# The last quarter of a merged product turned by token tile, and the loads around it: a hybrid encoder block on one core

## The chip, the cores and the metric

The kernel runs on one core of one Trainium2 chip, for a batch of 1, 256 tokens and a width of 2048, all in float32. The metric is the device time of one execution in microseconds (us), lower is better. The engines are PE (matrix multiply, with PEld for its weight loads), DVE (VectorE), ACT (ScalarE), POOL (GpSimd, which here only issues DMAs) and SP (SyncE, which issues the loads of the weights). DMAs that ACT issues have a queue of their own too.

## The reference

One encoder block: two branches work side by side on the projected input (a gated linear attention, GLA, and a Hyena long convolution), sigmoid gates merge them, one product and a LayerNorm follow, then a squared-ReLU MLP and a second LayerNorm. The change lies between the merge and the first LayerNorm.

```python
proj = h @ w_in[l]
q, k, v, r, af, ab, hy_u, gate_logits = jnp.split(proj, split_idx, axis=-1)
y_gla = _gla_branch(q, k, v, r, af, ab, ...)
y_hy = _hyena_branch(hy_u, ...)
g = jax.nn.sigmoid(gate_logits).reshape(B, L, N_BRANCH, D)
merged = g[:, :, 0, :] * (y_gla @ w_gla_o[l]) + g[:, :, 1, :] * (y_hy @ w_hy_o[l])
mix = merged @ w_out[l]
h = _layernorm(DEEPNORM_ALPHA * h + mix, ln1_g[l], ln1_b[l])
ff = jnp.square(jax.nn.relu(h @ w_ff1[l])) @ w_ff2[l]
h = _layernorm(DEEPNORM_ALPHA * h + ff, ln2_g[l], ln2_b[l])
```

## The kernel before

Every large product is made of weight blocks of 128 x 2048 numbers (1 MB). `fetch` (line 115) loads a block on SP's queue into one of three `raw` tiles and splits it in two halves into a high and a low part: the high part `whi` is a cast on ACT (line 108), the low part `wlo` a subtraction on DVE (line 109). There are three slots each for halves of `whi` and `wlo`. Activations are kept as high and low parts as well, and three matmuls (high by high, high by low, low by high) make one exact product. `next_block` fetches one block and hands out an earlier one, so that two blocks are on their way.

`token_group` (line 215) makes one group of 512 output columns for both token tiles (tb = 0 and 1, of 128 tokens each): four blocks, each with four slices of the contraction, and for each slice three matmuls for tb = 0 and three for tb = 1, which is 96 matmuls in a group. After each block it calls `pump`. `later(d, fn)` (line 135) puts work aside until d more blocks have gone by; `pump` then runs it, and `drain` runs all that is left.

The place of the change is the product with `w_hy_o`, the groups ho0 to ho3 of lines 822 to 833. Each group is merged with the gates: a multiplication (line 828) and an addition (line 829) for each token tile on DVE. The result has tokens on the partitions, and the next product, with `w_out` (groups wo0 to wo3, lines 904 to 910), needs channels there, so it is turned: DVE transposes blocks of 32 x 32 (line 203), one DMA from POOL's queue writes the 512 KB of the group to DRAM (`bounce_out`, line 207, tensor tr_m), and four DMAs from the same queue read it back in the turned order (`bounce_in`, line 213, tile mg, 128 KB each). `back_split` (line 817) splits the tile mg into the high and low parts of mT, on ACT and DVE. For ho0 to ho2 this split is put aside for two blocks; for ho3 it comes at once, by `drain` on line 834, and so stands in the program ahead of the first block of wo0. The fourth block of each wo group reads the quarter of mT that ho3 gives.

Behind it the program loads x into z1 (line 842, 2 MB in one DMA) and the two LayerNorm rows, broadcast to all partitions, into rows1 (`load_rows`, lines 844 to 848 and 893, two DMAs of 1 MB), all on ACT's queue. They lie in the place that yhT (the input of the ho groups) had, so they can't start before the last ho matmul is done. `add_mix` (line 895) reads z1 after each wo group, and rows1 is read from line 930 on. Lines 957 to 1006 are an order written out by hand for the LayerNorm. `load_rows(2)` on line 1062, behind `ff1(0)`, loads the rows of the second LayerNorm into the same tile.

The order of the instructions on each engine is not that of the program text: a planner goes through a simulated time, and gives an engine that is free the earliest instruction of the program whose inputs are ready by its estimates. What it has put in line stays in line on the chip. `tc.high_priority()` moves instructions ahead of others that are ready at the same time.

Of the kernel before, what the change touches and what calls it, by code (L numbers as in the profile page):

```python
# [10 lines left out]
F32 = mybir.dt.float32  # L11
# [3 lines left out]
ALU = mybir.AluOpType  # L15
DRAM = bass.MemoryType.DRAM

P = 128
D = 2048
L = 256  # L20
NT = L // P
# [38 lines left out]
def block_kernel(  # L60
# [23 lines left out]
    nc = tc.nc  # L84
# [10 lines left out]
    base = ctx.enter_context(tc.tile_pool(name="base", bufs=1))  # L95
# [39 lines left out]
    def later(d, fn):  # L135
        clock[1] += 1
        side.append((clock[0] + d, clock[1], fn))
# [9 lines left out]
    def drain():  # L147
        for e in sorted(side, key=lambda e: e[:2]):
            e[2]()
        side.clear()  # L150
# [51 lines left out]
    def turn_blocks(st, src):  # L202
        nc.vector.transpose(st, src.rearrange("p k (b i) -> p b k i", b=4))  # L203

    def bounce_out(name, st, n):
        td = drp.tile([n, P, 512], F32, tag=f"tr_{name}", name=f"tr_{name}")
        nc.gpsimd.dma_start(td.rearrange("t p x -> p t x"), st)  # L207
        return td

    def bounce_in(sg, td):  # L210
        src = td.rearrange("t (a i) (b x) -> b i (t a) x", a=4, b=4)
        for b in range(4):
            nc.gpsimd.dma_start(sg[32 * b:32 * b + 32], src[b])

    def token_group(act, name):
        pss = [psum_main(f"{name}_{tb}") for tb in range(NT)]
        for b in range(4):
            token_products(pss, act, [next_block()], range(NT), b)
            pump()
        return pss  # L220
# [28 lines left out]
    dfth = base.tile([P, 4, P], F32R, tag="dfth", name="dfth")  # L249
    dftl = base.tile([P, 4, P], F32R, tag="dftl", name="dftl")  # L250
# [11 lines left out]
    with tc.tile_pool(name="xp", bufs=1) as xp:  # L262
# [26 lines left out]
        for g in range(4):  # L289
            pieces = 2 if g == 0 else 1  # L290
            for b in range(OPENING):
                if g % 2 == 0:
                    halves_of[b] = weight_half(b, g // 2)
                hi, lo = halves_of[b]
                n = pieces if b == 0 else 1
                w, step = 512 // n, 4 // n
                for i in range(n):
                    at = 512 * (g % 2) + w * i
                    cs = slice(512 * g + w * i, 512 * g + w * (i + 1))
# [150 lines left out]
    pa = open_ps[0]  # L450
# [18 lines left out]
    for g in range(4):  # L469
        ng = fp.tile([P, 512], F32, tag="ng", name=f"ng{g}")  # L470
        nc.scalar.dma_start(ng, norm_g[0:1, g * 512:(g + 1) * 512].broadcast_to([P, 512]))
        pss = token_group(xT, f"r{g}")
# [181 lines left out]
    def m_part(g, tb):  # L654
        return m_sb[g // 2][:, tb, (g % 2) * 512:(g % 2 + 1) * 512]
# [160 lines left out]

    def back_split(dst, sg):
        src = sg.rearrange("p a (k j) -> p k a j", k=4)
        hi, lo = (dst[:, :, i].rearrange("p k (a j) -> p k a j", a=8) for i in range(2))
        split_hi_lo(hi, lo, src)  # L820

    for g in range(4):
        pss = token_group(yhT, f"ho{g}")
        st = hp.tile([P, NT, 512], F32, tag=("Z", "pa")[g % 2], name=f"mt{g}")
        for tb in range(NT):
            gp2 = g2_sb[:, tb, g * 512:(g + 1) * 512]
            mp = m_part(g, tb)
            nc.vector.tensor_tensor(gp2, gp2, pss[tb], op=ALU.mult)
            nc.vector.tensor_tensor(mp, mp, gp2, op=ALU.add)
            turn_blocks(st[:, tb].rearrange("p (b k j) -> p b k j", b=4, k=4), mp.rearrange("p (k x) -> p k x", k=4))  # L830
        sg = hp.tile([P, 8, P], F32, tag=("Tl", "pb")[g % 2], name=f"mg{g}")
        bounce_in(sg, bounce_out(f"m{g}", st, NT))
        later(2, lambda g=g, sg=sg: back_split(mT[:, 4 * g:4 * g + 4], sg))
    drain()
    hstk.close()
    qkg.close()

# [1 line left out]
    ep = ctx.enter_context(tc.tile_pool(name="ep", bufs=1))  # L839
    zr = base.tile([P, 4, D], F32, tag="yT", name="zr")  # L840
    z1 = zr[:, 0:2]
    nc.scalar.dma_start(z1, x.rearrange("(a p) d -> p a d", p=P))

    def load_rows(i0):
        rows = zr[:, 2:4]
        for i in range(2):
            nc.scalar.dma_start(rows[:, i, :], ln_rows[i0 + i:i0 + i + 1, :].broadcast_to([P, D]))
        return rows
# [41 lines left out]
                            MM(ps, sl, hi[:, cs], start=False, stop=(kt == KT - 1))  # L890

    st1 = ep.tile([P, NT, 8, 6], F32, tag="bst", bufs=2, name="bst1")
    rows1 = load_rows(0)

    def add_mix(ps, tb, at, n):
        zc = z1[:, tb, at:at + n]
# [338 lines left out]
```

## Time and profile before

| what | value |
|---|---|
| median of 3 runs | 1858.11 us (1857.54 to 1872.73) |
| profiled execution, its own time | 1857.15 us |
| its span in the trace | 1855.3 us |
| PE busy | 1834.9 us, 99% of the span |
| DVE busy | 1311.4 us, 71% |
| ACT busy | 913.8 us, 49% |
| POOL busy | 177.7 us, 10% |
| moved by DMA | 411.64 MB, 222 GB/s on average |

The profile is one execution. Busy times of the engines overlap, so they don't add up to the span. The chain of waits follows the work that ended last back from the end of the execution, and the windows give the busy time of each engine, the granted clock of PE (1.00 is full speed) and the load of the DMA engines in a stretch. Times within the execution are counted from the start of the span.

### The profile page before, as it was taken

Reading aid. Unit: us, or ns where it says so; the run is one execution under the profiler, and the core shown is the slowest. Engines: PE = TensorE matmul, PEld = TensorE weight load, DVE = VectorE, ACT = ScalarE, POOL = GpSimd, SP = SyncE. Lnnn points to the kernel's source line nnn. Section 1 sums busy time; section 2 is a strip of 40 time slices with the busy share of each in tenths; the row PEclk is TensorE's granted clock in tenths of the full one; section 3 lists DMA queues with packets and bytes.
Section 4 is the critical chain, followed back from the end, with each engine's and each line's share of the span. In section 5 each row is a group of like instructions: output and inputs, shape, how many; then the busy total and the mean of one; then the engine's idle time right before and its main releaser. Section 6 shows DMA issues by size and latency. Waiting matters only on the chain.

```text
span 1855.3 us, 22858 instructions
## 1 busy us (share of the span) xinstructions
PE 1834.9 (99%) x8732; PEld 1531.8 (83%) x8732; DVE 1311.4 (71%) x1660; ACT 913.8 (49%) x1152; POOL 177.7 (10%) x316
## 2 busy tenths in 40 slices
PE   8999999999999999999999899999999999999998
PEld 6888888888888888888888687888888888888887
DVE  6778878985798899898756566666655655565567
ACT  5555547665555555555544344444434443444332
POOL 1000000031111121121101100011100100010000
PEclk9999999999999999999999999999999999999999
DMA  8667665457666676676666863677755765676553
GB/s 283 217 231 283 241 241 184 176 182 238 220 222 232 221 258 228 228 243 239 231 215 227 309 214 116 243 234 245 235 196 197 248 226 191 221 233 222 187 197 120
DMA packets 73582, 411.64 MB, mean 222 GB/s; under 512 B 10912, under 2 KB 13632, under 8 KB 34048
## 3 DMA queue, kind: packets, MB, share of 16 engines
q1 hardware_dynamic: 47376, 324.03, 48.6%
q0 software_dynamic: 19328, 66.88, 11.8%
q10 hardware_dynamic: 6768, 19.27, 3.0%
q8 instruction: 68, 1.11, 0.2%
q14 instruction: 42, 0.34, 0.1%
HBM read 375.01 MB, written 35.13 MB: 221 GB/s over the span
## 4 chain that ended last, share of the span: by engine, by line
PE 59%; issue 4%; DMA 3%; DVE 2%; POOL 1%; ACT 0%; DVEq 0%; ACTq 0%; POOLq 0%
PE w L93 19%; PE f L93 18%; PE g L93 5%; PE go L93 4%; PE wo L93 3%; PE ux L93 2%; PE uz L93 2%; PE uv L93 2%; DMA tr_m<-mt 1%; PE ho L93 1%; PE Zp L93 1%; PE yp L93 1%; DMA mg<-tr_m 1%; PE wo L49 0%; PE f L49 0%
## 5 line engine op out<-in xcount | busy, mean ns | idle before, releaser
L109 DVE TENSOR_TENSOR wlo<-raw,whi 128x1024 fp32r<-128x1024 f32 (+2 forms) x603 | 726.2, 1208 | 408.6 <-ACT whi L108 398.2
L108 ACT CAST whi<-raw 128x1024 fp32r<-128x1024 f32 (+2 forms) x603 | 628.0, 1043 | 710.1 <-PE w L93 185.1
L93 PE MATMUL w<-whi,f 128*128 128x512 f32 x960 | 296.1, 389 | 0.0
L93 PE MATMUL f<-whi,hT 128*128 128x512 f32 x960 | 296.1, 389 | 0.0
L93 PEld LDWEIGHTS f<-whi,hT 128*128 128x128 f32 x960 | 180.2, 188 | 37.4
L93 PEld LDWEIGHTS w<-whi,f 128*128 128x128 f32 x960 | 180.2, 188 | 37.4
L93 PE MATMUL f<-wlo,hT 128*128 128x512 f32 x480 | 186.7, 389 | 0.0
L93 PE MATMUL w<-wlo,f 128*128 128x512 f32 x480 | 186.7, 389 | 0.0
L93 PE MATMUL g<-whi,xT 128*128 128x512 f32 x512 | 158.3, 389 | 0.0
L93 PEld LDWEIGHTS g<-whi,xT 128*128 128x128 f32 x512 | 96.1, 188 | 20.0
L93 PEld LDWEIGHTS w<-wlo,f 128*128 128x128 f32 x480 | 90.1, 188 | 18.7
L93 PEld LDWEIGHTS f<-wlo,hT 128*128 128x128 f32 x480 | 90.1, 188 | 18.6
L93 PE MATMUL g<-wlo,xT 128*128 128x512 f32 x256 | 99.9, 390 | 0.0
L93 PE MATMUL r<-whi,xT 128*128 128x512 f32 x256 | 82.3, 391 | 0.0
L93 PE MATMUL v<-whi,xT 128*128 128x512 f32 x256 | 80.1, 390 | 0.0
L93 PE MATMUL go<-whi,yg 128*128 128x512 f32 x256 | 79.8, 389 | 0.0
L93 PE MATMUL ho<-whi,yh 128*128 128x512 f32 x256 | 79.0, 389 | 0.0
L93 PE MATMUL wo<-whi,mT 128*128 128x512 f32 x208 | 67.0, 401 | 5.0 <-ACT whi L108 3.7
L93 PE MATMUL uz<-xT,whi 128*128 128x512 f32 x256 | 65.0, 392 | 0.0
L93 PE MATMUL uv<-xT,whi 128*128 128x512 f32 x256 | 64.8, 391 | 0.0
L93 PE MATMUL ux<-xT,whi 128*128 128x512 f32 x256 | 64.6, 392 | 0.0
L207 POOL DMA_DIRECT2D tr_f<-work x15 | 10.9, 725 | 523.2 <-DVE work L203 523.2
(343 smaller groups left out, 2844.1 us busy)
## 6 DMA issues: line engine op xcount, KB each, us to landing
raw<-wblk SPq DMA_DIRECT2D x302, 1024.0 KB, 4.9
Td<-T POOLq DMA_DIRECT2D x16, 768.0 KB, 4.5
Tl<-Td POOLq DMA_DIRECT2D x16, 768.0 KB, 4.8
w<-w4s ACTq DMA_DIRECT2D x16, 512.0 KB, 5.1
tr_f<-work POOLq DMA_DIRECT2D x15, 512.0 KB, 3.7
back<-tr_f POOLq DMA_DIRECT2D x60, 128.0 KB, 4.1
zr<-ln_rows ACTq DMA_DIRECT2D x4, 1024.0 KB, 10.8
raw<-wblk SPq DMA_DIRECT2D x11, 256.0 KB, 7.5
```

The lines of the kernel that those rows point to most:

```text
L93: return eng.tensor.matmul(*args, **kw)
L108: nc.scalar.copy(hi, src)
L109: nc.vector.tensor_tensor(lo, src, hi.bitcast(F32), op=ALU.subtract)
L207: nc.gpsimd.dma_start(td.rearrange("t p x -> p t x"), st)
```

## The change

- Group ho3 leaves the loop. `merge` holds the two DVE operations and the transposition for one token tile; for ho0 to ho2 it does what the loop did.
- For ho3 the merge of each token tile is given high priority, and has a tile of its own (tags pa and zf). The turned result of one token tile goes out in one DMA of 256 KB, and comes back in four DMAs of 64 KB, into a tile that takes the place of dfth or dftl.
- The split of the first token tile is put aside for one block, that of the second for two: they stand in the program behind the first and the second block of wo0, and not ahead of it.
- x is loaded in four pieces of 512 columns, put aside for 0, 3, 6 and 9 blocks; the rows of the first LayerNorm are put aside for 8.

```diff
     def back_split(dst, sg):
         src = sg.rearrange("p a (k j) -> p k a j", k=4)
-        hi, lo = (dst[:, :, i].rearrange("p k (a j) -> p k a j", a=8) for i in range(2))
+        hi, lo = (dst[:, :, i].rearrange("p k (a j) -> p k a j", j=32) for i in range(2))
         split_hi_lo(hi, lo, src)
 
-    for g in range(4):
+    def merge(g, tb, ps, st):
+        gp2 = g2_sb[:, tb, g * 512:(g + 1) * 512]
+        mp = m_part(g, tb)
+        nc.vector.tensor_tensor(gp2, gp2, ps, op=ALU.mult)
+        nc.vector.tensor_tensor(mp, mp, gp2, op=ALU.add)
+        turn_blocks(st.rearrange("p (b k j) -> p b k j", b=4, k=4), mp.rearrange("p (k x) -> p k x", k=4))
+
+    for g in range(3):
         pss = token_group(yhT, f"ho{g}")
         st = hp.tile([P, NT, 512], F32, tag=("Z", "pa")[g % 2], name=f"mt{g}")
         for tb in range(NT):
-            gp2 = g2_sb[:, tb, g * 512:(g + 1) * 512]
-            mp = m_part(g, tb)
-            nc.vector.tensor_tensor(gp2, gp2, pss[tb], op=ALU.mult)
-            nc.vector.tensor_tensor(mp, mp, gp2, op=ALU.add)
-            turn_blocks(st[:, tb].rearrange("p (b k j) -> p b k j", b=4, k=4), mp.rearrange("p (k x) -> p k x", k=4))
+            merge(g, tb, pss[tb], st[:, tb])
         sg = hp.tile([P, 8, P], F32, tag=("Tl", "pb")[g % 2], name=f"mg{g}")
         bounce_in(sg, bounce_out(f"m{g}", st, NT))
         later(2, lambda g=g, sg=sg: back_split(mT[:, 4 * g:4 * g + 4], sg))
+    pss = token_group(yhT, "ho3")
     drain()
+    for tb in range(NT):
+        with tc.high_priority():
+            st = hp.tile([P, 512], F32, tag=("pa", "zf")[tb], name=f"mt3{tb}")
+            merge(3, tb, pss[tb], st)
+        sg = base.tile([P, 4, P], F32, tag=("dfth", "dftl")[tb], name=f"mg3{tb}")
+        bounce_in(sg, bounce_out(f"m3{tb}", st[:, None, :], 1))
+        later(1 + tb, lambda sg=sg, tb=tb: back_split(mT[:, 12:16, :, tb * P:(tb + 1) * P], sg))
     hstk.close()
     qkg.close()
 
@@
-    nc.scalar.dma_start(z1, x.rearrange("(a p) d -> p a d", p=P))
+    for g in range(4):
+        cs = slice(g * 512, (g + 1) * 512)
+        later(3 * g, lambda cs=cs: nc.scalar.dma_start(z1[:, :, cs], x[:, cs].rearrange("(a p) d -> p a d", p=P)))
 
@@
-    rows1 = load_rows(0)
+    rows1 = zr[:, 2:4]
+    later(8, lambda: load_rows(0))
```

## Rows read from the trace of the kernel before

**Rows 1.** The page's first part: busy us, share of the span, instructions of each engine

```profile
PE 1834.9 (99%) x8732; PEld 1531.8 (83%) x8732; DVE 1311.4 (71%) x1660; ACT 913.8 (49%) x1152; POOL 177.7 (10%) x316
```

**Rows 2.** Chain of waits (start us, us, what), one later feed-forward stretch

```profile
1408.24 87.04 PE f L93 x384
```

**Rows 3.** Windows: PE, PEld, DVE, ACT, POOL busy, PE's clock, DMA share, GB/s

```profile
1035.50:1054.80 19.30, 17.08 (x73) 13.36 (x72) 14.17 (x15) 10.04 (x10) 0.72 (x1) 1.00 0.94 378
1054.80:1068.00 13.20, 9.17 (x23) 6.35 (x24) 4.91 (x5) 5.13 (x5) 2.33 (x4) 0.74 0.73 246
1068.00:1117.30 49.30, 49.30 (x219) 40.79 (x218) 33.24 (x40) 22.79 (x22) 0.00 (x0) 1.00 0.62 216
```

**Rows 4.** Timeline of PE (start us, us; in brackets idle before, and releaser)

```profile
1035.28 0.39 PE L93 MATMUL ho<-whi,yh 128*128 128x512 f32 x1
1037.13 0.73 PE L93 MATMUL wo<-whi,mT 128*128 128x512 f32 x2 [1.47 <-ACT whi L108]
...
1054.38 0.39 PE L93 MATMUL wo<-whi,mT 128*128 128x512 f32 x1
1055.90 0.73 PE L93 MATMUL wo<-whi,mT 128*128 128x512 f32 x2 [1.14 <-ACT whi L108]
...
1064.45 0.79 PE L93 MATMUL wo<-whi,mT 128*128 128x512 f32 x1 [1.27 <-ACT mT L108]
```

**Rows 5.** Timeline of ACT around the end of ho3 (ACTq: its DMA issues)

```profile
1035.09 1.04 ACT L108 CAST mT<-mg 128x1024 fp32r<-128x1024 f32 x1 [6.49 <-DMA mg<-tr_m]
1035.71 0.39 ACTq L842 DMA_DIRECT2D zr<-x  x1
```

**Rows 6.** Timeline of DVE after the end of ho3

```profile
1036.17 1.22 DVE L109 TENSOR_TENSOR mT<-mg,mT 128x1024 fp32r<-128x1024 f32 x1 [6.31 <-ACT mT L108]
1037.31 2.35 DVE L109 TENSOR_TENSOR wlo<-raw,whi 128x1024 fp32r<-128x1024 f32 x2
1039.58 1.28 DVE L828 TENSOR_TENSOR g_sb<-g_sb,ho 128x512 f32<-128x512 f32 x2
1040.78 1.29 DVE L829 TENSOR_TENSOR m<-m,g_sb 128x512 f32<-128x512 f32 x2
...
1043.12 1.30 DVE L203 STREAM_TRANSPOSE mt<-m 128x512 f32<-128x512 f32 x2
```

**Rows 7.** Chain of waits from ho0 to wo0: the way through DRAM

```profile
974.43 3.78 DMA tr_m<-mt
...
982.83 5.25 DMA mg<-tr_m
...
1044.71 9.81 DMA tr_m<-mt
...
1055.05 1.74 POOL mg L213 x3
1056.79 6.46 DMA mg<-tr_m
```

**Rows 8.** DMA issues, whole span: count, KB each, median us to landing

```profile
tr_y<-yt POOLq DMA_DIRECT2D x8, 256.0 KB, 3.6
```

**Rows 9.** DMA issues, the same view of 1036 to 1075 us

```profile
zr<-ln_rows ACTq DMA_DIRECT2D x2, 1024.0 KB, 14.1
```

**Rows 10.** Tile ng (a row of gates): duration min/median/max, first and last start

```profile
L476 DVE TENSOR_TENSOR g_sb<-sr,ng x8: 681/688/693, 161.9 to 261.3; 128x512 f32<-128x512 f32 x8
L471 ACTq DMA_DIRECT2D ng<-norm_g x4: 334/334/339, 64.9 to 229.0; - x4
```

**Rows 11.** Timeline of ACT at the end of the first LayerNorm

```profile
1151.73 0.33 ACTq L847 DMA_DIRECT2D zr<-ln_rows  x1
```

**Rows 12.** Tile yb (a turned GLA tile of one token tile): its split

```profile
L108 ACT CAST yg<-yb x8: 616/622/624, 397.8 to 434.6; 128x512 fp32r<-128x512 f32 x8
L109 DVE TENSOR_TENSOR yg<-yb,yg x8: 681/692/694, 398.5 to 435.3; 128x512 fp32r<-128x512 f32 x8
```

## The prediction

> **What bounds the kernel now.** I read the page first. PE is busy for 99% of the span [rows 1], so nothing off PE's path can be worth much, and a gain can only come from the places where PE stands idle or runs slowly. A list of PE's waits by stretch led to the change from ho to wo, so I asked for the windows around it. The price of a matmul at full pace comes from a long undisturbed stretch: 384 in 87.04 us, 0.2267 us each [rows 2]. From the end of ho3 (its last matmul starts at 1035.28 [rows 4], so about 1035.5) to 1117.3, PE makes 13 blocks of w_out, 312 matmuls, which are 70.7 us of work. It takes 81.8. The 11.1 us between are all that the change can win here, 0.6% of the time.
>
> They fall in two places [rows 3]. In the first window three blocks (72 matmuls, 16.3 us) take 19.3: 3.0 lost. The third window is full at clock 1.00, and what it leaves of the other 240 matmuls (54.4 us) is 5.1 us of work in the middle window, which lasts 13.2: 8.1 lost. Of these PE was idle for 4.0 (13.20 less 9.17), and 4.1 went to work at a lower granted clock (0.74 on average, a mix of the two levels 1.2 and 2.4 GHz; PE had just stood still when it fell).
>
> The timelines say why. At the start of wo0 PE waits for a cast of weights on ACT [rows 4], and ACT had stood for 6.49 us before the split of **ho2's** quarter, whose data came late [rows 5]. At 1054.8 three blocks of wo0 are done. PE fills in some matmuls of wo1 from 1055.90, and goes on with wo0's fourth block only at 1064.45, when **ho3's** quarter is cast [rows 4]. The chain back from there [rows 7]: read landed about 1063.3, read issued from 1055.05, written from 1044.71 to 1054.52, and before that DVE: the merge begins at 1039.58, behind the low part of ho2's quarter and two `wlo`, and another `wlo` (1041.98) cuts in between the additions and the transpositions, which end at 1044.42 [rows 6]. The write took 9.81 us where that of ho0 took 3.78 [rows 7]: the 4 MB of x and rows were issued from 1035.71 on [rows 5], the rows took 14.1 us to land [rows 9], and the DMA engines were 94% busy over the window [rows 3].
>
> **The change part by part.** All sums are against the profiled execution's 1857.15 us (span 1855.3 and 1.85 around it).
>
> *The first 3.0 us stay.* Nothing before the end of ho3 is changed: ho2's quarter takes the same way, and ACT waits for it until 1035.09.
>
> *The merge by token tile.* The two `wlo` of 1037.31 were put in line before ho3 had ended, and ho2's low part stands ahead of them, so priority can't overtake either: the merge still begins at 1039.58. An operation is half of a pair, 0.65 us [rows 6]. Three for the first tile end at 1041.5, the second tile's at 1043.5, without a `wlo` between. The issue follows 0.3 us behind (1044.42 to 1044.71): the first write goes at 1041.8, 2.9 us earlier than before, the second at 1043.8, 0.9 earlier. The `wlo` that is overtaken ends at 1044.7 and not 1043.2. It serves the second block of wo0, which starts two blocks (10.9 us) before 1054.8, at 1043.9, and reads it 0.3 to 0.5 us later: a cost between 0 and 0.6, I take 0.3.
>
> *The loads put aside.* The text says later, but the planner gives a free ACT any load whose place is free. Two rows show it. The gate row ng stands in the program right before the first r group; its first use is at 161.9, and its load was issued at 64.9 [rows 10]. The rows of the second LayerNorm stand behind ff1(0); they were issued at 1151.73, when the first LayerNorm had just let go of their tile [rows 11] and that stage had hardly begun. All six loads become possible at the end of ho3, and ACT is idle for half of the window (10.04 busy of 19.30 [rows 3]). So I expect them within a few us of 1035.7 again, with the same 4 MB. Three more issues of about 0.39 us [rows 5] are hidden in ACT's idle time; were that gone, they would cost 1.2. Were the loads really late, z1's first piece would still have the 21.8 us of wo0.
>
> *The way through DRAM, first tile.* The write of 256 KB costs between 3.6 (the median of that size [rows 8]) and 9.81 (the whole, under the loads [rows 7]). I add half of the extra of the whole, 3.0, to 3.6: 6.6, landed at 1048.4. POOL issues 0.53 later, each of four reads takes it 0.58, so the last goes at 1050.7. From there a landing took 5.25 (ho0) to 6.46 (ho3) [rows 7]; I take 6.0: 1056.7. The cast of half a quarter is 0.62 [rows 12]: PE may start at 1057.3.
>
> The Trainium skill has a price for the DMAs alone (DMA: Bandwidth & Descriptors, Anatomy of one DMA, SWDGE path): about 2.0 us fixed plus the bytes at 436 GB/s, as an estimate 2.6 us for this write and 2.2 for a read. By it the first tile would be there before 1050, and the time that of the first rival. The trace disagrees where loads run: by the same formula the whole write is 3.2 us, against 3.78 and 9.81.
>
> *Second tile.* Written at 1043.8 behind the first on the same queue, so I take 8.0 of 6.6 to 9.81: 1051.8. POOL is free by then, the last read goes at 1054.1, lands at 1060.1; cast and low part (0.62 and 0.69 [rows 12]) are done at 1061.4.
>
> *PE.* It is idle from 1054.8 to 1057.3, 2.5 us, then has 24 matmuls of the first tile, 5.4 us. One pause in place of two should cost half of the 4.1 lost at the lower clock, 2.0. So the first tile ends at 1064.7, and the second is waiting by then. The splits put aside cost nothing: ACT and DVE are half idle. The resident block x0, whose cast waited for ho3's split to free its place, can only come earlier.
>
> *Sum.* Lost after the change: 3.0 + 0.3 + 2.5 + 2.0 = 7.8, against 11.1. That is 3.3 less: 1853.85 for a profiled execution. The median of the runs lies 0.96 above that execution, so 1854.8.
>
> *Both ends.* With 3.6 and 5.25, the first tile is cast at 1053.5 and the second at about 1056; nothing is lost behind 1054.8, the gain is 7.8 to 8.1, and the time 1850. With 9.81 and 6.46, the first tile is cast at 1061.0: 6.2 idle, 4.1 slow and 3.3 make 13.6, and the time 1860.6.
>
> **The rivals.** *Short way* (15%): the loads do come later, or don't hurt transfers of half the size. For it: 3.78 without loads [rows 7]. Against it: rows 10 and 11. 1850.
>
> *Halves travel no faster than the whole* (20%): the change does not do what it says, since the time on the way is latency and queueing. With 9.81, 6.46 and a single pause, 3.3 + 6.2 + 2.0 = 11.5: 1858.5. For it: a write of 256 KB took 3.6 at the median [rows 8], one of 512 KB 3.78. Against it: the write leaves 2.9 us earlier. The Trainium skill speaks for this rival: the same page (Bandwidth, Measured) advises batches of 1 MiB or more, and here one write and four reads become two and eight. In the section Queues, rings and completion order it says that each DMA engine takes the queues in turn, packet by packet; the 9.81 under loads agrees.
>
> *Slower: PE takes both tiles slice by slice* (20%). If the planner thinks both tiles are there when the fourth block's turn comes, it keeps the program's order, in which each slice of the contraction has the first tile's three matmuls, then the second's. PE then stands until the **second** tile is cast, and nothing of wo1 fills the gap. It loses from the point where that cast ends after 1060.6 (1054.8 plus 11.1 - 3.3 - 2.0). My middle value is 1060.7; with the high prices (the last read issued at 1056.1, landed at 1062.6) 1063.2, 3.3 + 8.4 + 4.1 = 15.8 and 1862.8. Between them, 1860.5. Against it: the planner did fill a gap with wo1 [rows 4], so it saw ho3's quarter come late, and would see the first tile come first.
>
> **How the numbers follow.** My forecast has 45%, with a range of its own from 1852.5 to 1857.5. From the short way to half of the slower rival, 1849.5 to 1860.5 leaves out the upper half of that rival, 10%, and something for what I don't see. Over 1% is 18.6 us, about what a measurement of this kernel can tell from no change. All that PE loses here is 11.1, so faster by that much has 1%; slower would take an order that starves PE elsewhere, 3%; within 1%, 96%.
>
> **What the profile would show.** Two writes and eight reads of tr_m at about 1041.8, 1043.8 and from 1048.9, with landings near 6.6 and 8; six loads on ACT's queue within 5 us of 1035.7; PE's first wait at 1037.1 as before; and a single gap from 1054.8 to about 1057.3, then the first tile's matmuls alone. Loads that start only from 1045 on would speak for 1850. A gap that ends with the second tile's cast, or a `wlo` or cast of weights that stands behind a late split, would speak for the slower end. The forecast is wrong if the merge begins long before 1039, if ho2's quarter no longer holds ACT, or if another stretch than this one moves by more than 2 us.

## The result and the profile after

The changed kernel takes 1865.96 us (median of 20 runs, 1861.51 to 1875.94), the kernel before 1859.16 in the same comparison (20 runs). The ratio is 1.0035, with a 95% interval from 1.0020 to 1.0049. So it is slower by some 6.5 us, within 1%, where I had forecast 1854.8: the time lies above my range and on the other side of the kernel before.

The profiled execution's span is 1861.3 us against 1855.3. Cut at two points, the end of ho3 and the first matmul that uses the resident blocks of w_out, the 6.0 us are: 1.8 less ahead of the first (the same instructions in both), 2.8 more between them (84.7 against 81.9), and 5.0 more behind the second (742.9 against 737.9). PE's part of the page, then the windows from the end of ho3 on, columns as in [rows 3]:

```profile
PE 1836.9 (99%) x8732; PEld 1532.4 (82%) x8732; DVE 1310.7 (70%) x1661; ACT 913.2 (49%) x1153; POOL 179.5 (10%) x321
```

```profile
1034.00:1054.90 20.90, 18.49 (x72) 14.50 (x72) 14.25 (x15) 10.06 (x11) 5.12 (x10) 0.92 0.95 374
1054.90:1068.50 13.60, 8.30 (x21) 5.28 (x22) 5.92 (x6) 5.02 (x6) 0.39 (x1) 0.75 0.58 161
1068.50:1118.30 49.80, 49.80 (x221) 41.22 (x220) 32.30 (x39) 22.68 (x22) 0.00 (x0) 1.00 0.63 223
```

Of the 2.8 us between the points, 1.6 lie in the first window: 20.90 us in place of 19.30, with PE's granted clock at 0.92 on average (a mix of the levels 1.2 and 2.4 GHz, behind PE's waits of 2.5 us at the start of wo0) where it had been 1.00. That need not be the change's doing: again_before, a second profile of the kernel before (below), takes 20.3 us at 0.92 there. In the middle window PE stands for 5.3 us where it had stood for 4.0. The timelines of POOL, ACT and PE (start, us, what; in brackets the idle time before, and its releaser) show the way of ho3's quarter:

```profile
1042.64 1.15 POOL L207 DMA_DIRECT2D tr_m<-mt  x2 [17.58 <-DVE mt L203]
...
1050.68 2.20 POOL L213 DMA_DIRECT2D mg<-tr_m  x4 [6.89 <-DMA tr_m<-mt]
```

```profile
1062.22 1.99 ACT L108 CAST xh<-raw 128x1024 fp32r<-128x1024 f32 x2 [6.28 <-DMA raw<-wblk]
1064.12 0.61 ACT L108 CAST mT<-mg 128x512 fp32r<-128x512 f32 x1
1064.64 1.05 ACT L108 CAST whi<-raw 128x1024 fp32r<-128x1024 f32 x1
1065.59 0.61 ACT L108 CAST mT<-mg 128x512 fp32r<-128x512 f32 x1
```

```profile
1064.79 0.60 PE L93 MATMUL wo<-whi,mT 128*128 128x512 f32 x1 [3.68 <-ACT mT L108]
```

PE waits for the cast of the first token tile, and that cast has no wait of its own: ACT was standing before something else, the cast of xh, the high part of the resident block x0 of w_out, whose weights landed at 1062.12. In the kernel before they landed late too, at 1061.30; but there the cast of x0 stood behind the split, and here it stands ahead of it. The last read of the first tile had landed at 1059.09, 5.0 us before its cast, and that of the second at 1061.74. The chain of waits (start, us, what) goes through the weights, and no longer through DRAM as in [rows 7]:

```profile
1054.52 7.60 DMA raw<-wblk
...
1062.22 1.05 ACT xh L108
...
1063.30 0.92 DVE xl L109
1064.21 0.53 ACT mT L108
```

Of the 5.0 us behind, nearly all lie in one place. Windows of the feed-forward part at equal distances from the first resident matmul, the kernel before first; x in the first column counts the matmuls:

```profile
1197.40:1357.40 160.00, 160.00 (x708) 132.48 (x707) 96.50 (x92) 75.28 (x78) 20.64 (x34) 1.00 0.71 240
...
1437.40:1537.40 100.00, 100.00 (x443) 82.81 (x442) 57.78 (x56) 46.11 (x47) 11.50 (x19) 1.00 0.69 235
```

```profile
1198.40:1358.40 160.00, 160.00 (x707) 132.48 (x707) 96.31 (x92) 75.20 (x78) 20.58 (x34) 1.00 0.73 241
...
1438.40:1538.40 100.00, 97.39 (x422) 79.83 (x421) 55.88 (x54) 43.42 (x45) 11.46 (x19) 0.98 0.68 225
```

The turned quarters of the feed-forward part come in three stretches: seven of ff1(0) and ff1(1), called the first group below; four of ff1(2), called the third group; and four of ff1(3). In the 100 us of the third group 21 matmuls fewer are made, 4.8 us at 0.2267 each [rows 2]. The order of the instructions on every engine is the same there in both kernels. ACT, kernel before and after, at the casts of the turned quarters (tile f) there:

```profile
1447.71 1.05 ACT L108 CAST f<-back 128x1024 fp32r<-128x1024 f32 x1 [3.02 <-DMA back<-tr_f]
1468.58 1.05 ACT L108 CAST f<-back 128x1024 fp32r<-128x1024 f32 x1 [2.12 <-DMA back<-tr_f]
```

```profile
1449.30 1.05 ACT L108 CAST f<-back 128x1024 fp32r<-128x1024 f32 x1 [3.65 <-DMA back<-tr_f]
1474.35 1.04 ACT L108 CAST f<-back 128x1024 fp32r<-128x1024 f32 x1 [6.92 <-DMA back<-tr_f]
```

The same pattern as around wo0: a cast that waits for a DMA stands ahead of casts of weights in ACT's line. Below, the times between the two points are called the stretch, those behind the second the tail; a list of every kernel's stands at the end of the experiments.

### The profile page after: what moved, and what is told of

Read it like the earlier page. It is cut to its first block, busy times and chain, and to the rows that moved or that the text cites. A ratio compares the mean times of both kernels' runs of the same rounds, so it can differ in the third digit from the quotient of the medians.

```text
span 1861.3 us, 22875 instructions
## 1 busy us (share of the span) xinstructions
PE 1836.9 (99%) x8732; PEld 1532.4 (82%) x8732; DVE 1310.7 (70%) x1661; ACT 913.2 (49%) x1153; POOL 179.5 (10%) x321
## 4 chain that ended last, share of the span: by engine, by line
PE 59%; DMA 3%; issue 3%; DVE 2%; ACT 1%; POOL 0%; DVEq 0%; ACTq 0%; POOLq 0%
PE w L93 19%; PE f L93 18%; PE g L93 5%; PE wo L93 4%; PE go L93 4%; PE ux L93 2%; PE uz L93 2%; PE uv L93 2%; PE ho L93 1%; PE Zp L93 1%; PE yp L93 1%; DMA mg<-tr_m 1%; DMA tr_m<-mt 1%; DVE wlo L109 0%; DMA back<-tr_f 0%
```

## The experiments

Each ratio is to the kernel before, run on the same chip, with a 95% interval.

**The change once more, and its two halves.** again_after is the changed kernel as it is. split_only is the change with the old loads, loads_only the kernel before with the new ones.

```diff
# split_only: the change, but
-    for g in range(4): ... later(3 * g, ... dma_start(z1[:, :, cs], ...))
+    nc.scalar.dma_start(z1, x.rearrange("(a p) d -> p a d", p=P))
-    later(8, lambda: load_rows(0))
+    rows1 = load_rows(0)
# loads_only: the kernel before with the lines marked - above in place of those marked +
```

> The changed kernel once more, for a second profile. In the first profile the way from the end of ho3 to the first matmul of the resident block took 84.3 us (before: 81.8), and another 4.8 us were lost in the third feed-forward quarter, where ACT waited for data read back from DRAM. If x0's cast on ACT holds the split of ho3's tiles (theory A), the stretch is again 83.5 to 86, with PE's long wait put down to the split on ACT and the cast of x0 right before it. If the loss is an accident of that execution (rival), the stretch is 81 to 83 here. The loss in the feed-forward quarters has no cause in the change that I can see (the order on every engine is the same there), so I expect none or one elsewhere.

> The changed kernel with x and the rows loaded as before, so that only the turning by token tile and the move of its tiles are left. loads_only was as fast as the kernel before (1.0003). If the whole loss belongs to this half, the time is 1.003 to 1.005 of the kernel before, the stretch 84 to 88, and x0's cast stands ahead of the first split, waiting for its weights. If the two halves only lose together (pieces that keep the DMA engines busy until x0's weights are due), the time is within 0.1% of before and the stretch under 83.

> The kernel before with the loads of the change alone: x in four pieces and the rows put aside, ho3 as before. If the loads are put in line at the end of ho3 whatever the program says, as the prediction said, the six issues come within 8 us of the end of ho3 and the stretch is 81 to 83 as before, time within 2 us. If pieces of 2 KB a row slow the DMAs (rival C), the write of tr_m takes over 11 us and the stretch is 84 or more, 3 to 6 us slower. If they are really later, 76 to 79.

again_after: 1.0042 (1.0021 to 1.0063), 1866.5 us. xh waited 8.80 us this time, and PE 6.28. split_only: 1.0027 (1.0005 to 1.0049); loads_only: 1.0003 (0.9982 to 1.0023). So the loss goes with the split and not with the loads. In split_only ACT stands at the same place:

```profile
1061.44 1.99 ACT L108 CAST xh<-raw 128x1024 fp32r<-128x1024 f32 x2 [7.31 <-DMA raw<-wblk]
1063.34 0.61 ACT L108 CAST mT<-mg 128x512 fp32r<-128x512 f32 x1
```

The loads, put aside or not, were issued from 1034.57 to 1040.2 in loads_only, as predicted, and changed nothing.

**x0's cast, taken away from ho3's splits in two ways.** x0_behind ties it behind them (`behind(a, b)` gives a its place behind b, and no wait for data). place_back changes no order by hand: it gives the two read tiles the places in the Hyena pool that a whole quarter had, so that x0, which takes over the same places, can't be ready first.

```diff
# x0_behind (W_OUT_END - 3 is x0)
+                if first == W_OUT_END - 3:
+                    behind(last_split[0], m_split[0])   # its cast after the second split's
+                    behind(last_split[1], m_split[1])   # its low part too
# place_back
-        sg = base.tile([P, 4, P], F32, tag=("dfth", "dftl")[tb], name=f"mg3{tb}")
+        sg = hp.tile([P, 4, P], F32, tag=("pb", "Tl")[tb], name=f"mg3{tb}")
```

> The changed kernel with one more ordering: the cast and the low part of the resident block x0 are put in line behind the split of ho3's second tile, nothing else. Theory A (x0's cast, which waits for its weights from DRAM, stands in ACT's line before the split): the first tile is cast when its read has landed, at about 25 us after the end of ho3 and not 30.3; PE's long wait falls from 3.7 to 0 to 1.5, the stretch from 84.3 to 79 to 82, and the time falls by 3 to 6 us against the changed kernel, to about that of the kernel before. Rival B (halves travel no faster, eight reads are the cost): the cast moves by 1 us at most, the stretch stays at 83 to 85. Rival C (the loads in pieces are the cost): no change either, 84.

> The changed kernel with ho3's two read tiles in the places pb and Tl of the Hyena pool instead of those of dfth and dftl; nothing else. Theory A2 (x0's cast got ahead of the split only because moving the read tiles out of that pool let go of x0's place early): the planner now puts both splits before x0's cast by itself, and the time is that of x0_behind, 5 to 8 us under the changed kernel, 0 to 3 us from the kernel before; the stretch from the end of ho3 to the resident block is 79 to 82 us. Rival (the early place is not the reason, the later place of the splits in the program is): x0's cast still stands first and the stretch is 84 to 88 as in the two profiles of the changed kernel.

x0_behind: 1.0003 (0.9980 to 1.0026), 1859.4 us, 7 under again_after in the same comparison. place_back: 1.0005 (0.9988 to 1.0022), 1859.4 us. ACT in place_back, where the reads of the first tile had landed at 1058.68:

```profile
1058.78 0.62 ACT L108 CAST mT<-mg 128x512 fp32r<-128x512 f32 x1 [3.10 <-DMA mg<-tr_m]
1062.42 0.62 ACT L108 CAST mT<-mg 128x512 fp32r<-128x512 f32 x1 [0.20 <-DMA mg<-tr_m]
1064.11 2.00 ACT L108 CAST xh<-raw 128x1024 fp32r<-128x1024 f32 x2 [1.07 <-DVE mT L109]
```

The planner itself puts the splits first here. So what let x0 ahead was the move of the read tiles out of the pool, and its price is 6 to 7 us (1.0003 and 1.0005 against 1.0035 and 1.0042). From the end of wo0's third block to the first resident matmul the change takes 63.5 us, x0_behind 60.2 and place_back 58.1. With x0's early place gone the change is worth nothing in total, though: not 3.3 us less. In this part these two profiles are some 2 us shorter on average than those of the kernel before (62.6, and again_before's 59.9), but the time behind the first resident matmul, below, is longer.

**What the loads cost the way through DRAM.** loads_held is x0_behind with all six loads held behind the second tile's cast; x0_behind_spread has each tied to a cast of weights, some blocks apart.

```diff
# loads_held, in short: the pieces of x put aside for two blocks more, and
+    behind(load, m_split[0])          # for each of the six
# x0_behind_spread
-        later(3 * g, lambda cs=cs: nc.scalar.dma_start(z1[:, :, cs], ...))
+        later((2, 4, 6, 10)[g], lambda cs=cs: behind(nc.scalar.dma_start(z1[:, :, cs], ...), last_split[0]))
+                later(8 + 3 * i, lambda i=i: behind(load_row(rows, i0, i), last_split[0]))
```

> As x0_behind, and the four pieces of x and the two rows are put in line on ACT behind the cast of the second tile, so that they are really later. Theory of the prediction (the loads slow the way through DRAM: 9.8 us for the write against 3.8): the two writes take 3.5 to 5 us and not about 8, the reads land 3 to 6 us earlier than in x0_behind, PE doesn't wait at the fourth block of wo0 or less than 1 us, and the stretch is 75 to 78, some 4 to 6 us under the kernel before. Rival (the way is latency, not load): the writes stay above 6, the stretch is within 1 us of x0_behind. A third way: the planner now expects the data so early that the casts stand too far ahead in ACT's line and hold weights; then PE waits for casts of weights, and the stretch is above 82.

> x0_behind with the loads of x and rows spread, each tied behind a cast of weights; ho2's split as in the kernel before. If the loads are what makes the writes of 8.7 us slow, the writes take 3 to 5 us here, PE waits at wo0's fourth block for under 1 us, and the 3 us at the start of wo0 stay: a stretch of 76 to 77 us, and 3 us under x0_behind, some 1855. If the loads only move the contention to the weights, PE waits for whi or wlo for 2 us or more behind wo0, and the stretch is 79 or more, with the time of x0_behind.

loads_held: 0.9989 (0.9966 to 1.0011); x0_behind_spread: 0.9999 (0.9982 to 1.0015). DMA issues of loads_held from 1034 to 1075 us (count, KB, median us to landing), and ACT afterwards:

```profile
tr_m<-mt POOLq DMA_DIRECT2D x2, 256.0 KB, 2.7
mg<-tr_m POOLq DMA_DIRECT2D x8, 64.0 KB, 5.1
```

```profile
1072.25 2.00 ACT L110 CAST whi<-raw 128x1024 fp32r<-128x1024 f32 x2 [7.41 <-DMA raw<-wblk]
```

Without the loads of x and rows beside it the write takes 2.7 us in place of 8.7, and both casts are done by 1056.1. So the loads of x and rows are what slows the writes, as I took it. But 4 MB that start at 1055.5 meet the weights, and ACT waits 7.41 us for those. (The estimate worked out for this write from the Trainium skill, DMA: Bandwidth & Descriptors, Anatomy of one DMA, SWDGE path, is 2.6 us; the 2.7 agrees.) With the loads spread over some blocks the writes take 2.7 us too, and PE still waits 4.1 us in all for `wlo` in wo.

**The first 3 us of the stretch.** ho2_behind is the kernel before with the split of ho2's quarter put off by one more block and held behind the casts of wo0's first block. all_three joins it with x0_behind and the spread loads, and was run twice; whole_spread is all_three without the turn by token tile.

```diff
-        later(2, lambda g=g, sg=sg: back_split(mT[:, 4 * g:4 * g + 4], sg))
+        later(3 if g == 2 else 2, lambda g=g, sg=sg: back_split(mT[:, 4 * g:4 * g + 4], sg, list(last_split) if g == 2 else None))
```

> The kernel before with the split of ho2's quarter put in line behind the casts of the first block of wo0, nothing of the change. In all five profiles ACT stands 6.2 to 6.8 us for ho2's data at the end of ho3, and PE loses 2.3 to 3 us at the start of wo0. If that wait is what holds the weights, PE starts wo0 without a wait, and the merge on DVE begins at 0.5 us after the end of ho3 and not at 4.1, so that the write leaves 3.5 us earlier: the stretch is 76 to 79 and the time 3 to 6 us under the kernel before. If the way through DRAM then takes so much longer (the write now meets all of the loads), the first wait goes and the second stays: 78 to 80, 1 to 3 us.

> The changed kernel with three orderings: x0 behind ho3's splits (x0_behind), ho2's split behind the casts of wo0's first block (ho2_behind), and the four pieces of x and the two rows each tied to a cast of weights near its own place in the program (2, 4, 6 and 10 blocks, rows at 8 and 11), so that they are spread over 60 us and not sent together. In loads_held the six together took the weights' turn instead (a cast waited 7.4 us for its block). Expected: writes 2.5 to 4 us, both tiles cast before the fourth block of wo0, no wait of PE over 1 us from the end of ho3 to the resident block, a stretch of 71.5 to 74 us, and 7 to 10 us under the kernel before (0.994 to 0.997). If spreading doesn't help, weights come late again and the stretch is 76 to 79.

> all_three once more, for a second profile. It lost some 12 us in the feed-forward part, where reads of the turned tiles took 7.8 to 9.9 us, though the stretch around wo0 was 8 us shorter. Theory A, chance of the single execution: this profile loses under 5 us there, and its span is near 1850. Theory B, a shift of the beat between the weights' loads and the turned tiles that comes with this order: over 8 us are lost there again, and a span near 1860. In both, the ratio to the kernel before is 0.996 to 0.999, and the stretch 73 to 75 us.

> The kernel before with its whole tile for ho3's quarter, with ho2's split behind the casts of wo0's first block, and the loads of x and rows spread, each tied behind a cast of weights. If the turn by token tile is worth something once its split stands in the right place, this kernel is slower than all_three by 2 to 3 us (the whole is written later and its split comes at once, some 3 us more of PE's idle time at wo0's fourth block). If it is worth nothing, the two are equal within 1 us: about 1853 to 1855.

ho2_behind: 0.9976 (0.9958 to 0.9995), 1855.1 us. Its ACT has 0.40 us of idle time where it had 6.49 [rows 5], and PE no wait at the start of wo0:

```profile
1032.05 1.05 ACT L110 CAST mT<-mg 128x1024 fp32r<-128x1024 f32 x1 [0.40 <-DMA mg<-tr_m]
```

all_three: 0.9974 (0.9955 to 0.9994), then 1.0000 (0.9983 to 1.0017) with a stretch of only 73.7 and 77.1 us. whole_spread: 0.9984 (0.9965 to 1.0002), with 4.0 us of waiting for ho3's quarter. whole_spread differs from all_three in the turn by token tile alone. In the stretch of these profiles that turn is worth 4 to 8 us (73.7 and 77.1 against 81.3), but the 2 to 3 us that I expected of it in the total are not to be seen, even where its splits stand right. And all_three's stretch, 3 to 8 us shorter than those of the kernel before, brought 4.8 us once (by the ratio; 1.9 by the medians) and nothing once: the rest goes in the tail, which takes 744.6 to 752.0 us in these three profiles.

**Why the tail grows.** In all nine profiles so far of kernels that split ho3's quarter the tail took 741.8 to 752.0; of the five that don't, only whole_spread took over 738.7. In the five, POOL pauses once for 1.26 us near 1440 us without a releaser that the profile shows. In the nine it stands 4.8 to 4.9 us ahead of the reads at that place, which I read as the usual wait with the same pause in it. POOL's issues in the kernel before, then in the change:

```profile
1434.17 0.72 POOL L207 DMA_DIRECT2D tr_f<-work  x1 [102.18 <-DVE work L203]
1438.31 0.60 POOL L213 DMA_DIRECT2D back<-tr_f  x1 [3.41 <-issue]
1440.16 1.74 POOL L213 DMA_DIRECT2D back<-tr_f  x3 [1.26 <-issue]
```

```profile
1435.13 0.72 POOL L207 DMA_DIRECT2D tr_f<-work  x1 [101.50 <-DVE work L203]
1440.72 2.32 POOL L213 DMA_DIRECT2D back<-tr_f  x4 [4.87 <-ACT whi L108]
```

Before, the pause falls behind the first read of the turned quarter; in the change, with five DMAs more on POOL's queue, ahead of it (4.87 where most other quarters have 3.3 to 3.7). The cast of f behind these reads then waits 3.4 to 4.1 us in the split kernels, 2.5 to 3.1 in the others. To test it, pad_before and pad_after add five tiny writes to POOL's queue, and x0_behind_pad and ho2_behind_pad do so in those kernels. f_behind and all_four instead put the cast of f one block later, in the change and in all_three.

```diff
# pad_*, behind ho3's reads (in the kernels with the change the source is st[:, 0:16])
+            for i in range(5):
+                td = drp.tile([P, 16], F32, tag=f"pad{i}", name=f"pad{i}")
+                nc.gpsimd.dma_start(td, st[:, 0, 0:16])
# f_behind, all_four
-            later(2, lambda g=g, sg=sg, f=f: back_split(f[:, 4 * g:4 * g + 4], sg))
+            later(3, lambda g=g, sg=sg, f=f: back_split(f[:, 4 * g:4 * g + 4], sg, list(last_split)))
```

> The kernel before with five tiny writes (128 x 16 numbers) more on POOL's queue behind ho3's reads, as many DMAs as the change adds there. In every profile POOL pauses for 1.26 us at one place near 1440 us: between the first and the second read of a turned quarter in the kernels that turn ho3's quarter whole, ahead of the first read in those that turn it by token tile, and there the first wait of that group is 3.4 to 4.1 us in place of 2.5 to 3.1. If the number of DMAs on POOL's queue sets the place of the pause, it falls ahead of the first read here too, the waits grow to over 5 us, and the time behind the first resident matmul is 741 to 744. If the pause stays between the reads, 738 to 739.

> The changed kernel with the same five tiny writes more on POOL's queue behind ho3's reads. If the number of DMAs sets the place of POOL's pause of 1.26 us, it moves by one more place, ahead of the write, where POOL has nothing to do for 100 us: the first wait of that group falls to 3 us or less, and the time behind the first resident matmul from 742.9 to about 738, with 4 us off the time of the change. If the place does not depend on it, 742 to 744 again.

> The changed kernel, with the split of every turned quarter of the feed-forward part put off by one block more and held behind the casts of that block's weights; nothing else is moved. Theory, that a second part of the loss lies in the feed-forward part: there the cast of the turned quarter (tile f) stands on ACT ahead of casts of weights, a first wait of over some 3.3 us delays these, the loads of the weights come in bunches, the next read is slower, and the waits grow (3.6, 6.9 in the profile of the change against 3.0, 2.1 before). With the cast further back the waits can't grow: the time from the first resident matmul to the end falls from 742.9 to 738 or less, and the kernel is 3 to 6 us faster than the change, near 1861. Rival, that these pauses have to do with the reads alone and not with the order on ACT: 742 to 745 again, and 1865.

> all_three with the split of every turned quarter of the feed-forward part put off by one block more and held behind the casts of that block's weights. all_three took 73.7 and 77.1 us around wo0, but 752 and 745 from the first resident matmul to the end, where the kernel before takes 738. If the order on ACT lets the waits grow there, the 8 us that were won around wo0 come through now: 738 or less, and 1848 to 1851, some 9 us under the kernel before. If not, 744 or more again, and 1855 to 1858.

> x0_behind (the changed kernel with the resident block's cast held behind the splits of ho3's quarter) with the five tiny writes on POOL's queue; the order on every other engine is that of x0_behind. If the two causes found make up the loss of the change, both are gone here: a stretch of 79 to 82 us as in x0_behind, a first wait under 1 us in the third feed-forward group, as in pad_before and pad_after, and 737 to 739 from the first resident matmul to the end, where x0_behind took 743.6: a time near 1855, some 10 us under the change and 4 under x0_behind. If the waits of the first feed-forward group grow, as in pad_after (from 3.2 us), 742 and no gain on x0_behind.

> ho2_behind (the kernel before with ho2's split held behind the casts of wo0's first block) with the five tiny writes on POOL's queue. ho2_behind and pad_before were each 4 us faster than before, the one by the stretch around wo0, the other by the pause that no longer meets the reads of a turned quarter. If the two gains add, 1850 to 1852. If pad_before's gain is chance, since its profile lost nothing in the feed-forward part and neither did that of before, 1854 to 1856.

> The kernel before once more, for a second profile. From the end of ho3 to the first matmul with the resident block it should take 81 to 83 us, as in the first profile (81.9). Theory A, that pauses of PE in the feed-forward part are chance of the single execution: this profile may show some too, up to 10 us in sum. Theory B, that they come with the change of the order around wo0: none here, under 2 us. Time: within 0.2% of the kernel before.

POOL in pad_before:

```profile
1325.71 1.75 POOL L213 DMA_DIRECT2D back<-tr_f  x3 [3.90 <-issue]
1328.50 0.58 POOL L213 DMA_DIRECT2D back<-tr_f  x1 [1.04 <-issue]
...
1434.02 2.32 POOL L213 DMA_DIRECT2D back<-tr_f  x4 [3.39 <-issue]
```

The pause moves, though not to where I expected it in pad_before: in all four padded kernels it comes two or three issues earlier, in the last quarter of the group before. There the first wait of the third group is 0.0 or 0.1, where it was 2.5 to 4.1 in the fourteen profiles above, and PE has no wait in the group. Windows of pad_after, at the distances of those above:

```profile
1200.90:1360.90 160.00, 156.41 (x683) 127.30 (x682) 92.28 (x90) 71.61 (x76) 20.59 (x34) 1.00 0.70 232
...
1440.90:1540.90 100.00, 100.00 (x443) 82.84 (x442) 59.56 (x56) 45.91 (x47) 12.18 (x20) 1.00 0.69 234
```

So what POOL's queue carries moves the pause, and with the pause gone from its quarters the third group's first wait is gone too. How the place follows isn't clear: POOL had issued 274 DMAs ahead of the pause in the kernel before, 278 in the change, 276 in pad_before and 281 in pad_after, so it isn't a fixed number of them. But pad_after now loses 24 matmuls, 5.4 us, in the first group, and x0_behind_pad and ho2_behind_pad lose there too. The waits on ACT for the casts of f in that group, one after the other, from its timelines:

| kernel | waits of the seven casts, us |
|---|---|
| before | 2.6, 1.1, 1.0, 0, 0.6, 0.2, 1.0 |
| pad_before | 2.5, 1.2, 0.9, 0, 1.5, 0.7, 2.7 |
| loads_only | 3.3, 3.4, 2.6, 0.5, 0.2, 1.3, 0 |
| again_after | 2.9, 3.4, 4.8, 6.7, 4.7, 5.2, 4.9 |
| pad_after | 3.2, 3.5, 4.5, 3.6, 5.1, 5.6, 5.3 |
| x0_behind_pad | 3.3, 5.3, 5.8, 5.9, 4.9, 5.8, 5.0 |

In the profiles with the f casts in their old place, a first wait of 2.3 to 2.6 us dies out (in the change and pad_before a wait of about 3 us comes back at the seventh cast), one from 2.7 to 3.3 may die out or grow. How waits may grow can be read from SP's issues of the weights in the change, behind the f cast that waited until 1449.30 and up to the one of 1474.35: 4.45, 5.44 and then 10.24 us apart, where an undisturbed row has 5.44 throughout:

```profile
1458.82 0.33 SPq L120 DMA_DIRECT2D raw<-wblk  x1
...
1463.27 0.33 SPq L120 DMA_DIRECT2D raw<-wblk  x1
...
1468.71 0.33 SPq L120 DMA_DIRECT2D raw<-wblk  x1
...
1478.95 0.33 SPq L120 DMA_DIRECT2D raw<-wblk  x1
```

My reading, from this one place: a late f cast holds the casts of weights behind it, their loads start late and close together, and the next read of a turned quarter (issued from 1464.29 on) runs beside two of them: its last part took 8.22 us in the chain of waits.

The times: pad_before 0.9978 (0.9958 to 0.9997), again_before 1.0009 (0.9990 to 1.0029), pad_after 1.0019 (1.0002 to 1.0037), x0_behind_pad 0.9990 (0.9968 to 1.0013), ho2_behind_pad 1.0012 (0.9990 to 1.0035), all_four 0.9996 (0.9976 to 1.0017), f_behind 1.0091 (1.0057 to 1.0125, six runs). The twelve times of ho2_behind_pad lie in two heaps, three from 1852 to 1855 and nine from 1862 to 1867; those of x0_behind_pad too, six up to 1857 and six from 1861. That is what a wait that either dies out or grows would give, with some 8 to 11 us between. f_behind and all_four, made to test that reading, fell as a cure: with the cast of f one block later the first four waits of the first group are 0.0 to 0.2 us, but they grow all the same by its end (2.9, 5.7 and 3.3, 6.9 in the last two quarters), and the tails are 745.4 and 744.5, as the rival in the expectation had it. The cast still stands ahead of the next block's casts there, so the reading isn't refuted by it, but it isn't shown either. Why f_behind is 10 us slower than the change isn't settled: its profile is of the fastest of its six executions (1869.33), and the stretch is 1.2 and the tail 2.5 us longer there than in the change's.

| kernel | stretch, us | tail, us | kernel | stretch, us | tail, us |
|---|---|---|---|---|---|
| before | 81.9 | 737.9 | ho2_behind | 80.2 | 738.5 |
| again_before | 80.4 | 738.7 | all_three | 73.7 | 752.0 |
| the change | 84.7 | 742.9 | all_three_again | 77.1 | 745.0 |
| again_after | 88.3 | 751.6 | whole_spread | 81.3 | 744.6 |
| split_only | 85.1 | 743.4 | x0_behind_spread | 79.0 | 743.5 |
| loads_only | 84.0 | 737.7 | f_behind | 85.9 | 745.4 |
| x0_behind | 80.7 | 743.6 | all_four | 73.5 | 744.5 |
| place_back | 78.9 | 741.9 | pad_before | 80.5 | 736.9 |
| loads_held | 79.0 | 741.8 | pad_after | 86.9 | 742.4 |
| x0_behind_pad | 81.5 | 747.7 | ho2_behind_pad | 82.0 | 746.4 |

Each is of one execution; x0_behind and place_back have tails 4 to 6 us longer than before in it, stretches 1 to 3 us shorter, and medians 1 and 2 us longer. The tails of single executions are no means.

## Why the prediction was wrong

**The step that failed** is the sentence on the resident block: "x0, whose cast waited for ho3's split to free its place, can only come earlier", costed at nothing. It did come earlier, and that is the loss. I asked what is late if a wait goes, but not what the freed instruction itself would wait for: its weights landed at 1062.12, and in ACT's line everything behind it, both splits among it, stood until then. That ACT is half idle on average didn't help: 6.28 us of its idle time were this wait, and the first tile's data lay there for 5.0 us. I had named the sign ("a `wlo` or cast of weights that stands behind a late split"), but the other way round: it was the split that stood behind a cast of weights. Two edits that put x0 behind again gave back 6 to 7 us, which is about the whole of the loss. The gain of 3.3 us that I had forecast on top is missing for other reasons, which follow.

**The merge by token tile** was mis-sized. I let the first write go 2.9 us earlier. Counted from the end of ho3 it went at 8.9 us in place of 9.2: the order on DVE is that of [rows 6], both tiles' multiplications, both additions, the `wlo` that I let be overtaken, then both transpositions:

```profile
1038.10 1.28 DVE L825 TENSOR_TENSOR g_sb<-g_sb,ho 128x512 f32<-128x512 f32 x2
1039.30 1.29 DVE L826 TENSOR_TENSOR m<-m,g_sb 128x512 f32<-128x512 f32 x2
1040.50 1.22 DVE L109 TENSOR_TENSOR wlo<-raw,whi 128x1024 fp32r<-128x1024 f32 x1
1041.64 1.30 DVE L203 STREAM_TRANSPOSE mt<-m 128x512 f32<-128x512 f32 x2
```

So the priority moved nothing here. Perhaps the planner fills the gap between an operation and the one that needs it with the other tile's; no run shows it.

**The way through DRAM** was right in its kind. The writes took 7.8 and 9.6 us (I had 6.6 and 8.0), the reads 6.5 at the median (6.0), and the first tile was there at 1059.1 (1056.7). That the write's price is the loads' is shown by the 2.7 us of loads_held. **The loads** came early as forecast: five of the six were issued within 3 us of the end of ho3, the last 7.4 us behind it, where I had said 5. **PE's pause** did not become one of two: it stood for 1.7 us around 1056 and for 3.7 before 1064.79. **The first 3.0 us** stayed, for the reason given, and were 4.6 in this profile, since the clock fell too (0.92, as in again_before). ho2_behind takes the wait at that place away, and is 2 us faster than before by the medians, 4.5 by the ratio. It, pad_before and the first run of all_three are the three whose intervals lay under 1; all_three's second run was at 1.0000, and the edits of the other two together, in ho2_behind_pad, brought nothing.

**The rivals.** None of the three has x0 in it. The one that was to end slower had PE take both tiles slice by slice; PE took up the block at 1064.79, before the cast of the second tile had begun (1065.59). Nearest comes the one in which halves travel no faster than the whole, for 1858.5: with x0 held back the change gives 1859.4, and the halves took 7.8 and 9.6 us to write. The nearness of the two times is in part luck, for a longer tail, which that sum doesn't hold, is in the 1859.4.

**What would make it wrong** named another stretch that moves by more than 2 us. One did: ff1's third group lost 4.8 us in the profile of the change, without an instruction of it in another order. That its first wait goes with the place of POOL's pause is shown by the padded kernels. What the pause is, why waits grow, and what decides in the first group whether a wait of about 3 us dies out or grows, stays open, and so does the share of each part in the median: one profile of a kernel is one draw.

## What to carry to other kernels

When an edit sets an instruction free, price the instruction in its new place: on an engine that takes its line in order, a cast that comes early but waits for a load holds everything behind it. A tile's place is a part of the order too; moving one to another pool can reorder an engine that the edit doesn't mention. And where a cast that waits for a DMA stands ahead of the casts that feed the next loads, small delays may feed themselves (growing waits are to be seen here, their cause isn't shown). Either way a gain won in one stage has to be looked for in the total, and the later stages counted in both profiles.

## What the hardware showed that was not expected

- POOL paused for 1.04 to 1.26 us at one place of its line (in the nine profiles above only as a wait that was longer by as much), and five tiny DMAs more moved that place. The Trainium skill (Runtime: NRT & Kernel Launch, Instruction fetch mechanics) says that an engine's instructions come in blocks by a queue of their own and calls the cost mostly hidden; a pause that moves with the number of instructions would fit such a block's end, but no run here shows that it is one: the DMA traces of 1432 to 1446 us hold no packet of the kind instruction in the kernel before or the change, where the pause falls in that window.
- The same 256 KB write took 2.7 us at the median where only loads of the weights were under way (loads_held), and 8.7 beside those and the loads of x and rows (the change).
- PE's granted clock was 0.64 to 0.75 on average (a mix of the levels 1.2 and 2.4 GHz) in the 13.6 us around wo0's fourth block in the change, whole_spread, pad_after and f_behind, where PE had stood there for 3.7 to 7.9 us, 1.00 in all_three, where it had stood for 1.6 us, and 0.87 in all_three_again, where it had for 3.9.
